# Six paired front pieces and a one-function 1/deviation tail in a one-layer decoder kernel

## The chip, the cores and the metric

The kernel runs on one core of a Trainium2 chip. The metric is the device time of one execution in microseconds (us); the figures here are the median of three runs. Engines are named as the profile names them: PE (TensorE matmuls; PEld its weight loads), DVE (VectorE), ACT (ScalarE), POOL (GpSimd) and SP (SyncE, which here only issues DMAs; ACT issues a few too).

## The reference

One layer of a decoder, for 256 prompt positions and 8 x 4 sample positions together (T = 288 columns), width D = 2048, in fp32:

```
z  = x @ w_in                       -> h, gate_b, gate_c, q, k, v, g_a, g_b
ya = gate_b * conv3(gate_c * h);  yb = merged dilated attention(q, k, v)
x1 = LN1(ALPHA*x  + (sigmoid(g_a)*(ya@w_a) + sigmoid(g_b)*(yb@w_b)) @ w_out)
y  = LN2(ALPHA*x1 + (silu(conv3(x1@w_up_a)) * (x1@w_up_b)) @ w_down)
LN(u) = (u - mean(u)) * rsqrt(var(u) + 1e-5) * g + b     over the 2048 features
```

The key and value caches and convolution states are outputs as well.

## The kernel before, in words

**Layout and products.** Activations lie feature-major: 128 partitions x 16 blocks of features (KD = 16) x 288 tokens. A weight block is 128 output features, 128x2048 fp32, 1 MiB in memory. Every fp32 product is made of three matmuls per 128x128 tile: operands are split into a rounded part (`hi`, a ScalarE cast) and the rest (`lo`, a VectorE subtraction), and `mms` (L188) adds hi·xh, hi·xl and lo·xh in PSUM. A block takes 48 matmuls of 288 columns.

**The stream of weights.** `prepare` (L161) issues a block's DMA on SP into `wst` (three buffers), and `half_block` (L134) casts (L137) and subtracts (L138) its two halves into `whi` and `wlo` (four buffers each). `product` (L174) takes a ready block, prepares the next and multiplies. The order on each engine is set by a scheduler that works from its own estimate of times; `tc.issue_after` and `behind` pin some instructions behind others.

**The front.** Twenty matmuls on zeros (L213) run while the first data come. x comes in four pieces (`FIRST`, L66: feature blocks 0-1, 2-7, 8-11, 12-15) by DMAs that ACT issues (L221); the first two weight blocks come in the same four pieces each, by DMAs that SP issues (L232), into two `wst` buffers. For every piece ACT casts and DVE subtracts the weights of each block (L234, L235) and x (L200, L201, in `split`). The product loop for q (L433) multiplies the first two blocks one after the other, interleaved by the scheduler. Behind the front's DMAs SP issues the third block, then constants (`cst`, `m_dist` into tile `yal`), the fourth block and parameters (`prm`), in the first three products (L436-438). A DMA carries one of eight completion semaphores in turn, so the ninth and later DMAs wait for the one eight places before.

**The tail.** The last products add into `dd`; `Norm.add` (L556) keeps sums of dd and of its square on POOL; two pairs of matmuls on a matrix of 1/D (L572, L573) spread mean and mean square over all partitions in PSUM (`p1`, `p2`). `finish_out` (L593) computes v = variance + eps (L600, DVE), then r = v^-1/2 as Ln (L608) and Exp (L609) on ACT, a Newton step (L614 ACT, L616 and L617 DVE, giving `dev` in PSUM) and a copy for POOL (L618). Over the 16 feature blocks it subtracts the mean (L604: blocks 0-8 on DVE in three passes, 9-15 on POOL), multiplies by dev (L604: 0-10 on DVE in four passes, 11-15 on POOL), and applies gain and bias (L630 on ACT for 0-8, 14, 15; L628 on DVE for 9-13). SP sends y in six pieces (L631). The first norm, `finish` (L578), uses the same Ln and Exp (L584, L585) and feeds the `w_up` products.

Of the kernel before, what the change touches and what calls it, by code (L numbers as in the profile page):

```python
# [11 lines left out]
F32R = mybir.dt.float32r  # L12
AF = mybir.ActivationFunctionType
ALU = mybir.AluOpType
# [3 lines left out]
P = 128  # L18
D = 2048
KD = D // P  # L20
# [6 lines left out]
H = T // 2  # L27
# [4 lines left out]
HK = KD // 2  # L32
# [18 lines left out]
C_M0 = C_TM + NT  # L51
# [11 lines left out]
N_CT = 18  # L63
N_REST = 48

FIRST = ((0, 2), (2, 6), (8, 4), (12, 4))  # L66

N_WARM = 20


N_STEP = N_CT + 2
N_STEP_BLOCKS = 2 * NG * NH + 5 * KD - 3

MEAN_DVE = ((0, 3), (3, 3), (6, 3))
MEAN_POOL = ((9, 1), (10, 2), (12, 2), (14, 2))
OUT_DVE = ((0, 1), (1, 3), (4, 3), (7, 4))
OUT_POOL = ((11, 1), (12, 2), (14, 2))
OUT_ORDER = ((0, 1), (1, 3), (4, 3), (7, 4), (11, 3), (14, 2))
OUT_LAST = (9, 10, 11, 12, 13)


@with_exitstack
def layer_kernel(ctx: ExitStack, tc: tile.TileContext, ins, outs):
    nc = tc.nc
    pe, dve, act, pool, sp = nc.tensor, nc.vector, nc.scalar, nc.gpsimd, nc.sync

    big = ctx.enter_context(tc.tile_pool(name="big", bufs=1))
    wp = ctx.enter_context(tc.tile_pool(name="wp", bufs=3))
    wk = ctx.enter_context(tc.tile_pool(name="wk", bufs=2))
# [8 lines left out]
    def sb(pl, shape, tag, dt=F32, bufs=None):  # L98
        return pl.tile(shape, dt, tag=tag, name=nm(tag), bufs=bufs)

    def acc(half=H):
        return sb(ps, [P, half, 2], "acc")

    def h2(ap):
        return ap.rearrange("p (h a) -> p h a", h=2)

    def h3(ap):
        return ap.rearrange("p k (h a) -> p k h a", h=2)
# [4 lines left out]
    def f32(ap):  # L113
        return ap.bitcast(F32)
# [3 lines left out]
    w_load = [None]  # L118
# [5 lines left out]
    def behind(i, after):  # L124

        tc.add_manual_dep(i.ins, after.ins.name, no_sync, reason="pace")
# [34 lines left out]
    def prepare():  # L161
        src, nk = next(w_left, (None, 0))
        if nk == 0:
            return
        st = sb(wp, [P, KD, P], "wst")
        d = sp.dma_start(st[:, :nk, :], src.rearrange("p (k c) -> p k c", c=P))
        loads[0] += 1
        n = loads[0]
        w_load[0] = d
        if n > NB_QKV + 5 * KD and n % 11 in (0, 4, 8):  # L170
            copy_rest(d)
        w_ready.append([half_block(st, k0, min(HK, nk - k0)) for k0 in range(0, nk, HK)])

    def product(x):  # L174

        w = w_ready.pop(0)
        if not w_ready:
            prepare()
        if steps_on[0]:
            spent[0] += N_STEP  # L180
            while spent[0] >= N_STEP_BLOCKS:
                spent[0] -= N_STEP_BLOCKS
                next(steps, None)
        o = acc(x[0].shape[-1])
        mms(o, w, x)
        return o.rearrange("p a h -> p h a")
# [12 lines left out]
    def split(hi, lo, src):  # L199
        act.copy(hi, src)  # L200
        dve.tensor_tensor(lo, src, f32(hi), ALU.subtract)  # L201
# [15 lines left out]
    xl = sb(big, [P, KD, 2, HX], "xl", F32R)  # L217
    x_in = ins["x"].rearrange("p (k t) -> p k t", t=T)
    xs = sb(big, [P, KD, T], "yah")
    for k0, n in FIRST:  # L220
        act.dma_start(xs[:, k0 : k0 + n, :], x_in[:, k0 : k0 + n, :])  # L221
    w_ready = []
    stage = []
    for b in range(2):
        stage.append((sb(wp, [P, KD, P], "wst"), ins["w_in"][b].rearrange("p (k c) -> p k c", c=P)))
        halves = [[sb(wp, [P, HK, P], n, F32R, bufs=4) for n in ("whi", "wlo")] + [HK] for _ in range(2)]
        w_ready.append(halves)
    for k0, n in FIRST:
        k = slice(k0, k0 + n)
        h = slice(k0 % HK, k0 % HK + n)  # L230
        for b, (st, src) in enumerate(stage):
            sp.dma_start(st[:, k, :], src[:, k, :])  # L232
            hi, lo, _ = w_ready[b][k0 // HK]
            act.copy(hi[:, h, :], st[:, k, :])  # L234
            dve.tensor_tensor(lo[:, h, :], st[:, k, :], f32(hi[:, h, :]), ALU.subtract)  # L235
            if b == 0:
                split(xh[:, k, :, :H], xl[:, k, :, :H], h3(xs[:, k]))
    x = (xh[:, :, :, :H], xl[:, :, :, :H])
    x_gb = (xh[:, :, :, :HG], xl[:, :, :, :HG])

    cst = sb(big, [P, C_M0], "cst")

# [187 lines left out]


    kv = sb(big, [P, 2, 2, NG, T], "dd")
    for j in range(NH):  # L433
        for g in range(NG):
            act.copy(h2(q_all[:, j, g]), product(x))
            if j == 0 and g > 0:  # L436
                for dst, src in ((cst, ins["cst"][:, :C_M0]), (m_dist, ins["cst"][:, C_M0:])) if g == 1 else ((prm, ins["prm"]),):
                    behind(sp.dma_start(dst, src), w_load[0])
        pool.tensor_copy(q_s[:, :, j, :], q_all[:, j, :, SEQ:])
    steps_on[0] = True  # L440
    for j in range(NH):
# [100 lines left out]
    class Norm:  # L542
# [13 lines left out]
        def add(self, i):  # L556
            d = dd[:, i]
            last = i == KD - 1
            q = self.s2 if i == 0 else sb(wk, [P, T], "cy", bufs=2)
            act.activation(q, d, AF.Square)  # L560
            if i == 0:
                pool.tensor_copy(self.s1, d)
            elif not last:
                pool.tensor_tensor(self.s1, self.s1, d, ALU.add)
                pool.tensor_tensor(self.s2, self.s2, q, ALU.add)
            if i == KD - 2:

                act.activation(lw[:, 3, 0:1], q[:, 0:1], AF.Ln)
            if last:
                self.p1, self.p2 = att(T), att(T)  # L570
                for p, s, e in ((self.p1, self.s1, d), (self.p2, self.s2, q)):
                    pe.matmul(p, ones_d, s, start=True, stop=False)  # L572
                    pe.matmul(p, ones_d, e, start=False, stop=True)  # L573
# [4 lines left out]
        def finish(self):  # L578

            mu, v, r, t = (lw[:, k] for k in range(3, 7))  # L580
            act.copy(mu, self.p1)
            act.activation(t, self.p1, AF.Square)
            dve.scalar_tensor_tensor(v, self.p2, EPS, t, ALU.add, ALU.subtract)
            act.activation(t, v, AF.Ln)  # L584
            act.activation(r, t, AF.Exp, scale=-0.5)  # L585

            dve.tensor_tensor(t, r, r, ALU.mult)
            dve.scalar_tensor_tensor(t, t, -0.5, v, ALU.mult, ALU.mult)
            dve.scalar_tensor_tensor(r, t, 1.5, r, ALU.add, ALU.mult)
            dve.scalar_tensor_tensor(mu, mu, -1.0, r, ALU.mult, ALU.mult)  # L590
            self.r, self.nmr = r, mu

        def finish_out(self, y, out):  # L593

            mu, r_pool, t = (lw[:, k] for k in range(3, 6))
            mean, v = self.p1, self.p2
            r, dev = (sb(ps, [P, T], tag, bufs=n) for tag, n in (("acc", None), ("long", 1)))
            act.activation(t, mean, AF.Square)
            act.copy(mu, mean)
            i_v = dve.scalar_tensor_tensor(v, v, EPS, t, ALU.add, ALU.subtract)  # L600

            def by_token(eng, k0, n, w, op):
                k = slice(k0, k0 + n)
                return eng.tensor_tensor(dd[:, k], dd[:, k], w.unsqueeze(1).broadcast_to([P, n, T]), op)  # L604

            for k0, n in MEAN_POOL:
                by_token(pool, k0, n, mu, ALU.subtract)
            act.activation(t, v, AF.Ln)  # L608
            act.activation(r, t, AF.Exp, scale=-0.5)  # L609
            with tc.issue_after(i_v.ins):  # L610
                for k0, n in MEAN_DVE:
                    i_m = by_token(dve, k0, n, mean, ALU.subtract)

            act.activation(t, r, AF.Square)  # L614
            with tc.issue_after(i_m.ins):
                dve.scalar_tensor_tensor(t, t, -0.5, v, ALU.mult, ALU.mult)  # L616
                i_r = dve.scalar_tensor_tensor(dev, t, 1.5, r, ALU.add, ALU.mult)  # L617
            act.copy(r_pool, dev)  # L618
            for k0, n in OUT_POOL:
                by_token(pool, k0, n, r_pool, ALU.mult)  # L620
            with tc.issue_after(i_r.ins):
                for k0, n in OUT_DVE:
                    i_m = by_token(dve, k0, n, dev, ALU.mult)
            for k0, n in OUT_ORDER:
                for i in range(k0, k0 + n):
                    if i in OUT_LAST:
                        with tc.issue_after(i_m.ins):
                            dve.tensor_scalar(y[:, i], dd[:, i], self.at(self.g, i), self.at(self.b, i), ALU.mult, ALU.add)  # L628
                    else:
                        act.activation(y[:, i], dd[:, i], AF.Identity, bias=self.at(self.b, i), scale=self.at(self.g, i))  # L630
                sp.dma_start(out[:, k0 : k0 + n, :], y[:, k0 : k0 + n, :])  # L631
# [267 lines left out]
```

## Time and profile before

| what | us |
|---|---|
| median of 3 runs (lowest to highest) | 1771.77 (1770.14 to 1772.48) |
| the profiled execution | 1772.71 |
| its span, first to last instruction | 1770.9 |
| PE busy in the span | 1749.3 (99%), 14277 matmul records |
| DVE, ACT, POOL busy | 1010.0, 800.8, 252.4 |
| mean granted TensorE clock | 0.995 of full speed |

The page gives busy time by engine, the chain of work that ended last, and the costliest groups by line. The trace behind it can be asked for the instructions of a stretch in order of time, for what an engine waited for, and for busy time, granted clock and DMA rate by stretch. Times within it count from the span's start. A busy PE is not a PE at its peak: a matmul's record is longer than the spacing of matmuls.

### The profile page before, as it was taken

Reading aid. Unit: us, or ns where it says so; the run is one execution under the profiler, and the core shown is the slowest. Engines: PE = TensorE matmul, PEld = TensorE weight load, DVE = VectorE, ACT = ScalarE, POOL = GpSimd, SP = SyncE. Lnnn points to the kernel's source line nnn. Section 1 sums busy time; section 2 is a strip of 40 time slices with the busy share of each in tenths; the row PEclk is TensorE's granted clock in tenths of the full one; section 3 lists DMA queues with packets and bytes.
Section 4 is the critical chain, followed back from the end, with each engine's and each line's share of the span. In section 5 each row is a group of like instructions: output and inputs, shape, how many; then the busy total and the mean of one; then the engine's idle time right before and its main releaser. Section 6 shows DMA issues by size and latency. Waiting matters only on the chain.

```text
span 1770.9 us, 33606 instructions
## 1 busy us (share of the span) xinstructions
PE 1749.3 (99%) x14277; PEld 1717.1 (97%) x14277; DVE 1010.0 (57%) x1321; ACT 800.8 (45%) x1178; POOL 252.4 (14%) x402
## 2 busy tenths in 40 slices
PE   8999999999999999999999999999999999999996
PEld 8999899999999999999999999999999999999996
DVE  4445446555645444455688787774555554555564
ACT  5444434333434333344455655553444443345444
POOL 0000000000000000001255233320011110011174
PEclk9999999999999999999999999999999999999998
DMA  8476677788787787467766566666666666666652
GB/s 305 172 301 258 258 292 272 288 304 316 260 322 301 296 322 264 151 247 270 283 218 235 214 226 226 226 226 223 229 227 226 230 222 233 219 236 219 242 191 104
DMA packets 59430, 436.25 MB, mean 246 GB/s; under 512 B 7184, under 2 KB 7696, under 8 KB 15248
## 3 DMA queue, kind: packets, MB, share of 16 engines
q1 hardware_dynamic: 57552, 428.22, 66.1%
q10 hardware_dynamic: 1728, 5.90, 0.9%
q8 instruction: 111, 1.82, 0.4%
q14 instruction: 39, 0.32, 0.0%
HBM read 389.89 MB, written 94.53 MB: 274 GB/s over the span
## 4 chain that ended last, share of the span: by engine, by line
PE 97%; ACT 1%; DVE 1%; DMA 0%; POOL 0%; issue 0%; ACTq 0%; DVEq 0%
PE acc L194 31%; PE acc L196 31%; PE acc L195 31%; PE long L356 1%; PE long L407 1%; DMA yah<-in_x 0%; PE att L283 0%; PE att L302 0%; ACT yah L630 0%; POOL qk_s L478 0%; DVE dd L604 0%; PE att L298 0%; ACT whi L137 0%; ACT xh L200 0%; PE att L276 0%
## 5 line engine op out<-in xcount | busy, mean ns | idle before, releaser
L138 DVE TENSOR_TENSOR wlo<-wst,whi 128x1024 fp32r<-128x1024 f32 (+1 forms) x580 | 710.5, 1225 | 608.0 <-ACT whi L137 602.1
L137 ACT CAST whi<-wst 128x1024 fp32r<-128x1024 f32 (+1 forms) x580 | 592.3, 1022 | 864.3 <-PE acc L195 763.6
L194 PE MATMUL acc<-xh,whi 128*128 128x288 f32 (+1 forms) x3264 | 940.1, 288 | 2.7 <-ACT whi L234 2.7
L196 PE MATMUL acc<-xh,wlo 128*128 128x288 f32 (+1 forms) x3264 | 937.3, 287 | 0.3 <-DVE wlo L235 0.3
L195 PE MATMUL acc<-xl,whi 128*128 128x288 f32 (+1 forms) x3264 | 936.3, 287 | 0.9 <-DVE xl L201 0.9
L194 PEld LDWEIGHTS acc<-xh,whi 128*128 128x128 f32 x3264 | 618.1, 189 | 14.0 <-issue 3.8
L196 PEld LDWEIGHTS acc<-xh,wlo 128*128 128x128 f32 x3264 | 618.1, 189 | 1.7 <-issue 0.8
L195 PEld LDWEIGHTS acc<-xl,whi 128*128 128x128 f32 x3264 | 618.3, 189 | 1.5 <-DVE xl L201 1.1
L194 PE MATMUL acc<-yah,whi 128*128 128x288 f32 x1216 | 348.2, 287 | 0.3 <-ACT yah L200 0.3
L196 PE MATMUL acc<-yah,wlo 128*128 128x288 f32 x1216 | 347.8, 286 | 0.0
L195 PE MATMUL acc<-yal,whi 128*128 128x288 f32 x1216 | 347.6, 286 | 0.0
L194 PEld LDWEIGHTS acc<-yah,whi 128*128 128x128 f32 x1216 | 229.7, 189 | 3.2 <-ACT h L519 2.5
L195 PEld LDWEIGHTS acc<-yal,whi 128*128 128x128 f32 x1216 | 229.8, 189 | 0.1
L196 PEld LDWEIGHTS acc<-yah,wlo 128*128 128x128 f32 x1216 | 229.8, 189 | 0.1
L478 POOL COPY qk_s<-u 128x2 f32<-128x2 f32 x44 | 41.7, 947 | 573.7 <-ACT u L680 441.5
L464 DVE SCALAR_TENSOR_TENSOR cy<-u,prm,cy 128x304 f32<-128x304 f32 x120 | 71.2, 594 | 3.3 <-ACT cy L462 0.6
L534 POOL TENSOR_TENSOR ya<-ya,dd 128x288 f32<-128x288 f32 x16 | 13.6, 849 | 306.0 <-DVE ya L533 306.0
L489 DVE TENSOR_TENSOR ya<-cy,acc 128x144 f32<-128x144 f32 x132 | 25.7, 249 | 33.0 <-PE acc L196 33.0
L478 POOL COPY cm<-u 128x2 f32<-128x2 f32 x16 | 3.0, 185 | 257.2 <-DVE u L505 257.2
L200 ACT CAST yah<-ya 128x288 fp32r<-128x288 f32 x76 | 32.7, 431 | 15.1 <-POOL ya L534 8.4
L201 DVE TENSOR_TENSOR yal<-ya,yah 128x288 fp32r<-128x288 f32 x76 | 34.9, 460 | 1.1 <-ACT yah L200 1.1
L462 ACT ACTIVATE cy<-u,prm 128x304 f32<-128x304 f32 x60 | 32.9, 549 | 3.1
(158 smaller groups left out, 791.8 us busy)
## 6 DMA issues: line engine op xcount, KB each, us to landing
wst<-in_w_in SPq DMA_DIRECT2D x114, 1024.0 KB, 6.1
wst<-in_w_up SPq DMA_DIRECT2D x88, 1024.0 KB, 4.8
wst<-in_w_down SPq DMA_DIRECT2D x32, 1024.0 KB, 4.9
cache<-in_ck SPq DMA_DIRECT2D x18, 1024.0 KB, 6.4
out_o_ck<-cache SPq DMA_DIRECT2D x18, 1024.0 KB, 9.2
cache<-in_cv SPq DMA_DIRECT2D x18, 1024.0 KB, 6.3
out_o_cv<-cache SPq DMA_DIRECT2D x18, 1024.0 KB, 9.9
wst<-in_w_a SPq DMA_DIRECT2D x16, 1024.0 KB, 4.9
```

The costliest lines, as they stand in the source:

```text
L137: act.copy(hi[:, :n, :], st[:, k0 : k0 + n, :])
L138: dve.tensor_tensor(lo[:, :n, :], st[:, k0 : k0 + n, :], f32(hi[:, :n, :]), ALU.subtract)
L194: pe.matmul(out, hi[:, c, :], xh_k, start=k == 0, stop=False)
L195: pe.matmul(out, hi[:, c, :], xl_k, start=False, stop=False)
L196: pe.matmul(out, lo[:, c, :], xh_k, start=False, stop=k == nk - 1)
L200: act.copy(hi, src)
L201: dve.tensor_tensor(lo, src, f32(hi), ALU.subtract)
L356: pe.matmul(p[j * NS : (j + 1) * NS], qm[:, j, b, :], c[:, o + j * cols : o + (j + 1) * cols], start=b == 0, stop=b == NB - 1,)
L462: act.activation(y, u[:, :YW], AF.Copy, scale=prm[:, w0 : w0 + 1])
L464: dve.scalar_tensor_tensor(y, u[:, i : i + YW], prm[:, w0 + i : w0 + i + 1], y, ALU.mult, ALU.add)
L478: pool.tensor_copy(dst[:, 0:2], u[:, SEQ : SEQ + 2])
L489: dve.tensor_tensor(a, b, c, ALU.mult)
```

## The change

In the front, x comes in six pieces (four of two feature blocks by ACT's DMAs, two of four by SP's), and both first weight blocks come together, one DMA for a piece of both, into one tile that borrows `dd`; hi goes into the tile `yal`, lo into two `cache` buffers. The casts and subtractions take both blocks at once. `first_two` multiplies piece by piece, term by term, alternating the two blocks, in an order that is pinned. The third block's load comes right behind the front's DMAs, and `cst`, `m_dist` and `prm` are issued three products later. There are 18 matmuls on zeros.

In the tail, r is one ACT function, `Abs_reciprocal_sqrt`, of v (in `finish` too), with the Newton step kept; its table is asked for where Ln's was. DVE's mean and dev passes take turns over the same blocks, and shares move: mean 0-7 on DVE and 8-15 on POOL; dev 0-11 on DVE and 12-15 on POOL; gain and bias 8-11 on DVE, the rest on ACT. The output pieces are 3, 3, 2, 4, 2 and 2 blocks.

In the compiled program the rest of the order on every engine is the same. On ACT the front's casts come in the order x0, w0, w1, x1, w2, x2, w3, x3, x4, w4, x5, w5 (w: both blocks of a piece), on DVE the subtractions likewise; on SP `cst` comes behind the fifth block, `m_dist` behind the sixth and waits for PE, `prm` behind the seventh. On ACT the tail's blocks come in the order 0-5, 12, 13, 6, 7, 14, 15.

```diff
-FIRST = ((0, 2), (2, 6), (8, 4), (12, 4))
-N_WARM = 20
+FIRST = ((0, 2, "act"), (2, 2, "act"), (4, 2, "act"), (6, 2, "act"), (8, 4, "sp"), (12, 4, "sp"))
+N_WARM = 18
-MEAN_DVE = ((0, 3), (3, 3), (6, 3))
-MEAN_POOL = ((9, 1), (10, 2), (12, 2), (14, 2))
-OUT_DVE = ((0, 1), (1, 3), (4, 3), (7, 4))
-OUT_POOL = ((11, 1), (12, 2), (14, 2))
-OUT_ORDER = ((0, 1), (1, 3), (4, 3), (7, 4), (11, 3), (14, 2))
-OUT_LAST = (9, 10, 11, 12, 13)
+NORM_DVE = ("m", 0, 3), ("r", 0, 3), ("m", 3, 3), ("r", 3, 3), ("m", 6, 2), ("r", 6, 2), ("r", 8, 2), ("r", 10, 2)
+MEAN_POOL = (8, 2), (10, 2), (12, 2), (14, 2)
+OUT_POOL = (12, 2), (14, 2)
+GB_DVE = (8, 9, 10, 11)
+OUT_ORDER = (0, 3), (3, 3), (6, 2), (8, 4), (12, 2), (14, 2)
...
-    for k0, n in FIRST:
-        act.dma_start(xs[:, k0 : k0 + n, :], x_in[:, k0 : k0 + n, :])
...
-            sp.dma_start(st[:, k, :], src[:, k, :])
-            hi, lo, _ = w_ready[b][k0 // HK]
-            act.copy(hi[:, h, :], st[:, k, :])
-            dve.tensor_tensor(lo[:, h, :], st[:, k, :], f32(hi[:, h, :]), ALU.subtract)
-            if b == 0:
-                split(xh[:, k, :, :H], xl[:, k, :, :H], h3(xs[:, k]))
+    w_two = sb(big, [P, 2, KD, P], "dd")
+    w_two_hi = sb(big, [P, 2, KD, P], "yal", F32R)
+    w_two_lo = [sb(wk, [P, 2, HK, P], "cache", F32R, bufs=2) for _ in range(2)]
+    w_in_two = ins["w_in"][0:2].rearrange("b p (k c) -> p b k c", c=P)
+    for k0, n, queue in FIRST:
+        k = slice(k0, k0 + n)
+        (act if queue == "act" else sp).dma_start(xs[:, k], x_in[:, k])
+        sp.dma_start(w_two[:, :, k], w_in_two[:, :, k])
+    for k0, n, _ in FIRST:
+        k = slice(k0, k0 + n)
+        split(xh[:, k, :, :H], xl[:, k, :, :H], h3(xs[:, k]))
+        split(w_two_hi[:, :, k], w_two_lo[k0 // HK][:, :, k0 % HK : k0 % HK + n], w_two[:, :, k])
+    def first_two():
+        prepare()
+        o = [acc() for _ in range(2)]
+        before = None
+        for k0, n, _ in FIRST:
+            for term in range(3):
+                for k in range(k0, k0 + n):
+                    xk = x[term == 1][:, k].rearrange("p h a -> p a h")
+                    for b in range(2):
+                        w = w_two_lo[k // HK][:, b, k % HK] if term == 2 else w_two_hi[:, b, k]
+                        i = pe.matmul(
+                            o[b], w, xk, start=k == 0 and term == 0, stop=k == KD - 1 and term == 2
+                        )
+                        if before is not None:
+                            behind(i, before)
+                        before = i
+        return [t.rearrange("p a h -> p h a") for t in o]
...
+    q_first = first_two()
-            act.copy(h2(q_all[:, j, g]), product(x))
-            if j == 0 and g > 0:
-                for dst, src in ((cst, ins["cst"][:, :C_M0]), (m_dist, ins["cst"][:, C_M0:])) if g == 1 else ((prm, ins["prm"]),):
-                    behind(sp.dma_start(dst, src), w_load[0])
+            act.copy(h2(q_all[:, j, g]), q_first.pop(0) if q_first else product(x))
+            if j == 1:
+                dst, src = ((cst, ins["cst"][:, :C_M0]), (m_dist, ins["cst"][:, C_M0:]), (prm, ins["prm"]))[g]
+                behind(sp.dma_start(dst, src), w_load[0])
...
-                act.activation(lw[:, 3, 0:1], q[:, 0:1], AF.Ln)
+                act.activation(lw[:, 3, 0:1], q[:, 0:1], AF.Abs_reciprocal_sqrt)
...
-            act.activation(t, v, AF.Ln)
-            act.activation(r, t, AF.Exp, scale=-0.5)
+            act.activation(r, v, AF.Abs_reciprocal_sqrt)
...
+            before = i_v
+            for n_op, (what, k0, n) in enumerate(NORM_DVE):
+                with tc.issue_after(before.ins):
+                    before = by_token(dve, k0, n, *((mean, ALU.subtract) if what == "m" else (dev, ALU.mult)))
+                if n_op == 0:
+                    with tc.issue_after(before.ins):
+                        dve.scalar_tensor_tensor(t, t, -0.5, v, ALU.mult, ALU.mult)
+                        before = dve.scalar_tensor_tensor(dev, t, 1.5, r, ALU.add, ALU.mult)
+                    act.copy(r_pool, dev)
```

## The prediction

> **What bounds the kernel now.** I read the page first, then PE's waits, then the first 30 us and the last 20 us in order of time. On the page:
>
> ```profile
> PE 1749.3 (99%) x14277; PEld 1717.1 (97%) x14277; DVE 1010.0 (57%) x1321; ACT 800.8 (45%) x1178; POOL 252.4 (14%) x402
> ...
> PE 97%; ACT 1%; DVE 1%; DMA 0%; POOL 0%; issue 0%; ACTq 0%; DVEq 0%
> ```
>
> PE is the bound, and between 30 and 1740 us its waits come to 0.3 us. So only the two ends can be shortened. ACT's casts that wait for PE's buffers start at 31.12 and 37.01, one block of 48 matmuls apart: 5.89 us, or 0.1226 us a matmul at full clock. PE's busy time and clock in the front, by the view of stretches (length, busy, count, clock, DMA share, GB/s):
>
> ```profile
> 4.60:8.00 3.40, 2.38 (x19) 1.00 1.02 417
> 8.00:11.40 3.40, 0.88 (x5) 0.98 1.02 409
> 11.40:14.75 3.35, 3.09 (x12) 0.50 1.05 387
> 14.75:18.10 3.35, 3.35 (x16) 0.50 1.01 413
> ```
>
> PE starves from 8 to 11.4, then works until 18.1 at half clock, 0.24 us a matmul, before it is back at full. The ACT and DVE rows beside it:
>
> ```profile
> 18.06 1.05 ACT L137 CAST whi<-wst 128x1024 fp32r<-128x1024 f32 x1 [1.96 <-DMA wst<-in_w_in]
> ...
> 25.37 0.40 ACT L435 COPY yah<-acc 128x288 f32<-128x288 f32 x1 [2.30 <-PE acc L196]
> ...
> 19.14 1.23 DVE L138 TENSOR_TENSOR wlo<-wst,whi 128x1024 fp32r<-128x1024 f32 x1 [1.27 <-ACT whi L137]
> ```
>
> L435 at 25.37 copies the second product. Its last matmul, the 96th, started about 0.3 us earlier (a matmul's record is 0.29 long), at 25.05. Had PE run at full clock without a gap, it would have begun at 25.05 - 95 x 0.1226 = **13.4**. I call this the equivalent start: what moves it moves the end. L137 and L138 show the other limit: the third block is in memory at 18.03, its first `lo` half ready at 20.37, when PE has not yet come to it.
>
> In the tail:
>
> ```profile
> 1755.74 1.28 ACT L609 ACT_TABLE_LOAD   x1
> ...
> 1757.11 1.04 DVE L604 TENSOR_TENSOR dd<-dd,att 128x864 f32<-128x864 f32 x1
> 1758.08 0.45 DVE L616 SCALAR_TENSOR_TENSOR cache<-cache,att 128x288 f32<-128x288 f32 x1
> 1758.56 0.46 DVE L617 SCALAR_TENSOR_TENSOR long<-cache,acc 128x288 f32<-128x288 f32 x1
> ...
> 1764.26 0.33 SPq L631 DMA_DIRECT2D out_o_y<-yah  x1
> ...
> 1765.00:1769.40 4.40, 0.00 (x0) 0.00 (x0) 0.00 (x0) 1.23 (x3) 0.00 (x0) 0.50 1.00 401
> ```
>
> Newton's step waits for DVE's third mean pass, not for the table: Exp and Square are done at 1757.89. At the end ACT's last block is done at 1766.23, but the queue writes without a gap from 1765.0 to 1769.4, and the span ends 1.5 later: the last four pieces, issued from 1764.26 on, are 12 blocks of 147 KB, 1.77 MB, 4.4 us at 401 GB/s. DMA ends the kernel, fed by the passes.
>
> **Front, step by step.** Bytes first. Third block and everything ahead of it are 2.36 (x) + 2.10 + 1.05 = 5.5 MB before and after; `cst` and `m_dist` were issued behind it and move further back. So it lands at 18.0 again, if short rows cost nothing. The first four paired pieces (1.05 MB) have 1 KB rows; the nearest row is the first output piece (1152-byte rows), 357 GB/s in its best 0.3 us against about 410: 0.0 to 0.4 us more. I take 18.2. Then ACT 1.05, DVE 1.23, handovers: first `lo` half at 20.55. PE can have done 98 matmuls by then; equivalent start 20.55 - 98 x 0.1226 = **8.5**.
>
> Is the rest ready? I share the measured rate between the queues by row length (2304 bytes of x to 1024 of w) and take 0.9 of it for the slowest part of a transfer; done for the kernel before, this gives 12.2 for the last x piece and 18.0 for the third block (ACT took them at 12.30 and 18.06). Estimated landings after: x0 4.1, w0 5.4, w1 7.7, w2 8.4, w3 9.2, x4 10.8, w4 12.3, x5 13.9, w5 15.3. ACT takes 0.67 (x) and 0.62 (w) for small pieces, 1.15 and 1.05 for large; DVE 0.76, 0.69, 1.35, 1.23 (rows of these sizes in L200, L201, L235, L137 and L138; 512 elements for w0-w3). ACT's order puts x1 behind w1, so x1, there at 5.3, is cast at 8.9. PE ends the six pieces at 7.6, 10.7, 12.2, 13.7, 16.6 and 19.5. That is 1.0 before block three's `lo`, so block three decides. Gain **13.4 - 8.5 = 4.9**. With the measured rate whole and no loss on short rows the same sum gives 7.2; with 0.87 and 15% loss, 9.3: gain 4.1 to 6.2.
>
> Two fewer matmuls on zeros: nothing, as PE then waits for w0 until 6.1 (about 0.25 us if it didn't). Matmuls, bytes and later weight loads are the same in number. `m_dist` now waits on SP until PE ends the pair (19.5), ahead of the seventh block and `prm`. The seventh block is due at 8.5 + 6 x 5.89 = 43.8 and takes about 8 us from issue: hidden, with some 15 us of cover; beyond that each us costs one. `prm` heads ACT's cast for that same block: same cover. The first norm loses a load and a pass (1.28 + 0.45 at 978 us); only DVE waited (1.1 us), PE didn't: 0.
>
> **Tail, step by step.** v is ready at 1755.28. Abs_reciprocal_sqrt has no row; ACT's passes over 288 elements take 0.39 to 0.44 without pointers and 0.63 with: I take 0.41. Square follows 0.45 later and ends at 1756.17, when DVE ends its first mean pass. Newton 0.94, copy 0.4: first dev pass at 1757.60 instead of 1759.48, **1.9 earlier**, with the mean passes of five blocks still to come. DVE in turn (3 blocks 0.96, 2 blocks 0.67 apart, 1.05 and 0.75 where the next waits for its result): blocks 0-2 done 1758.65, 3-5 1760.69, 6-7 1762.14, then 8-11 1763.48, gain and bias (0.34 apart, first 0.43) until 1764.95. Before: 1764.92. POOL has twelve blocks either way, 1.36 a pair: 12-13 at 1761.9, 14-15 at 1763.25. ACT at 0.52 a block: 0-2 until 1760.35, 3-5 1762.4, 12-13 1763.4, 6-7 1764.45, 14-15 1765.5: 0.75 earlier than before. The last three pieces are issued at 1764.5, 1764.95 and 1765.5; first bytes 0.8 after issue (as 1764.26 to 1765.07 before), 1.18 MB at 401 GB/s: 1768.2 against 1769.4. Gain **1.2**; 0.5 if each hand-over on DVE costs 0.2 more, 1.7 if the last piece finds the queue empty.
>
> On the table the row and a page differ. The trace has a load for Ln (L568) and one for Exp (L609), 1.28 us, and Exp starts 0.01 after the latter. The Trainium skill, page "ScalarE: Activation LUTs", section "What ACT_TABLE_LOAD costs", gives about 2.66 us with a drain, and its section "Table sets: the hidden batching unit" has Ln and Exp share one set. By 2.66 a removed load would be worth 1.4 us more than the row; the trace shows neither drain nor sharing.
>
> **The sum** is 4.9 + 1.2 = 6.1 against the profiled execution: 1772.71 - 6.1 = 1766.6. That execution lay 0.94 over the median; if all of this is profiling, 1765.7. Part of it may be the front's own stall, so I give **1766.0**.
>
> **Rivals.**
> - *The clock falls all the same.* In the four stretches above PE kept full clock after 70% busy, lost it after 26%, and didn't regain it after 92%. Afterwards PE is busy 43 to 63% in any 3.4 us between 5.2 and 11.4, in between, and full after. Half clock from 11.4 to 14.8 gives an equivalent start of 9.4, from 8 to 14.8 10.4, from 8 to 18.1 12.0: 1767 to 1769.5, middle 1768.3. The Trainium skill, page "TensorE: Matmul & The Clock Gate", section "Part 1: The HAM clock gate", has a free-running window of about 3.4 us, an idle one of which halves the clock. By it the phase differs from run to run, and no window here is idle. The trace agrees on the length (changes at 4.6, 11.4, 18.1).
> - *Slower: half clock through the whole front.* If the thin first pieces drop the clock at 5 us and gaps hold it down, 96 matmuls at 0.24 from 6.1 end at 29.1: equivalent start 17.8, and 13.4 - 17.8 + 1.2 = -3.2: 1775.0 with the 0.94 taken off, 1775.9 without. It decides if half clock lasts past about 23 us. Against it: from 10.6 on the casts feed PE faster than half clock eats.
> - *The tail gives nothing* (ACT's in-order 12-13 or DVE's turns late): 1767.2.
> - *The front doesn't get faster*, the paired loads with 1 KB rows running far under 350 GB/s: only the tail, 1770.6. For it: 103 to 210 GB/s between 2.4 and 3.6 us; against: over 340 from 4 us on with the same rows among them.
>
> **How the numbers follow.** Forecast 0.68, fallen clock 0.17, tail nothing 0.07, front nothing 0.04, slower 0.04. The measurement can tell about 0.2% (3.5 us) from no change: below 1768.2 is faster. The forecast, the tail rival and half of the fallen clock lie there: 0.80; slower by over 0.2% (1775.3) half of the slower rival, 0.02; same 0.18. The range, 1763.2 to 1769.2, takes 7.9 us (6.2 + 1.7) at the low end and the fallen clock's three-quarter point at the high.
>
> **What would show it.** Right: clock 1.00 throughout the front; first copy of q near 19.7 instead of 22.67; third block's first subtraction ending near 20.5 with PE waiting for it about 1 us; no table load between v and r; first dev pass 2.3 us after v; last block on ACT about 10.2 after v. Wrong: PEclk 0.5 anywhere before 20 us; weight pieces landing 1 us late or more; a PE wait on `whi` after 25 us; output pieces written with gaps at the end.

## The result and the profile after

The changed kernel takes **1766.56 us** (median of 8 runs, 1766.45 to 1766.66); the kernel before, measured beside it, 1771.49 (8 runs, 1769.95 to 1772.48). The ratio is 0.9973, 95% interval 0.9962 to 0.9984: 4.9 us less. The profiled execution after took 1766.61, with a span of 1764.8 and a clock of 0.997. Against the profiled execution before, 1772.71, that is 6.1, the sum of the prediction; against the medians it is 4.9. The difference comes from before: its runs lie 2.5 us apart, those after 0.2.

The page of the changed kernel, PE's busy time and the chain that ended last by engine:

```profile
PE 1747.1 (99%) x14275; PEld 1714.4 (97%) x14275; DVE 1009.9 (57%) x1321; ACT 797.5 (45%) x1175; POOL 253.8 (14%) x401
...
PE 97%; DMA 1%; ACT 1%; DVE 1%; POOL 0%; issue 0%; SPq 0%; ACTq 0%; DVEq 0%
```

PE is still the bound. The same four stretches of the front (length, PE busy, count, clock, DMA share, GB/s):

```profile
4.60:8.00 3.40, 3.12 (x19) 1.00 1.04 367
8.00:11.40 3.40, 2.73 (x16) 1.00 1.04 398
11.40:14.75 3.35, 3.29 (x27) 1.00 1.07 416
14.75:18.10 3.35, 3.35 (x30) 1.00 1.02 424
```

The hole from 8 to 11.4, 0.88 us busy before, is 2.73 busy now, and the two rows with 0.50 are gone. PE's rows in order of time (start, length from first to last, instruction, count, idle time before and who ended it):

```profile
5.92 0.80 PE L249 MATMUL acc<-xh,yal 128*128 128x288 f32 x4
...
7.97 0.76 PE L249 MATMUL acc<-xh,yal 128*128 128x288 f32 x4 [0.27 <-ACT xh L201]
...
10.64 0.76 PE L249 MATMUL acc<-xh,yal 128*128 128x288 f32 x4 [0.60 <-ACT xh L201]
...
18.91 1.14 PE L249 MATMUL acc<-xh,cache 128*128 128x288 f32 x8
19.89 0.29 PE L195 MATMUL acc<-xh,whi 128*128 128x288 f32 x1
20.01 0.29 PE L196 MATMUL acc<-xl,whi 128*128 128x288 f32 x1
20.35 0.39 PE L197 MATMUL acc<-xh,wlo 128*128 128x288 f32 x1
```

L249 is the pair, L195 to L197 the third block. The pair's 96 matmuls would take 11.8 us at 0.1226; they take 13.97, from 5.92 to 19.89. The 2.2 us more lie nearly all ahead of 11.5, in waits for ACT's casts of pieces 1 and 2 and the DVE subtractions behind them. At the third block's first `lo` PE loses 0.2 us. ACT and DVE beside it:

```profile
6.72 0.62 ACT L201 CAST yal<-dd 128x512 fp32r<-128x512 f32 x1 [0.86 <-DMA dd<-in_w_in]
7.25 0.67 ACT L201 CAST xh<-yah 128x576 fp32r<-128x576 f32 x1
9.39 0.62 ACT L201 CAST yal<-dd 128x512 fp32r<-128x512 f32 x1 [1.48 <-DMA dd<-in_w_in]
...
17.99 1.99 ACT L138 CAST whi<-wst 128x1024 fp32r<-128x1024 f32 x2 [1.45 <-DMA wst<-in_w_in]
19.97 0.70 ACT L452 COPY yah<-acc 128x288 f32<-128x288 f32 x2
...
19.07 2.36 DVE L139 TENSOR_TENSOR wlo<-wst,whi 128x1024 fp32r<-128x1024 f32 x2 [1.23 <-ACT whi L138]
```

Pieces are counted from 0. ACT can start on the weights of piece 1 (`yal<-dd`) at 6.72 and on those of piece 2 at 9.39; it stands idle before both, with x1 queued behind w1. It starts on the third block at 17.99; that block's first subtraction is the first half of the last row, done at 20.30. L452 copies the first product at 19.97 (22.67 before).

The tail, ACT and DVE from v on (L616 starts at 1749.85, takes 0.47 us and gives v at 1750.32):

```profile
1750.35 0.40 ACT L622 ACTIVATE acc<-att 128x288 f32<-128x288 f32 x1 [0.36 <-DVE att L616]
1750.77 0.41 ACT L623 ACTIVATE cache<-acc 128x288 f32<-128x288 f32 x1
...
1750.22 1.04 DVE L620 TENSOR_TENSOR dd<-dd,att 128x864 f32<-128x864 f32 x1
1751.22 0.46 DVE L633 SCALAR_TENSOR_TENSOR cache<-cache,att 128x288 f32<-128x288 f32 x1
1751.71 0.46 DVE L634 SCALAR_TENSOR_TENSOR long<-cache,acc 128x288 f32<-128x288 f32 x1
1752.63 1.05 DVE L620 TENSOR_TENSOR dd<-dd,long 128x864 f32<-128x864 f32 x1 [0.47 <-ACT cache L635]
```

And the stretch in which the last outputs are written (busy of PE, PEld, DVE, ACT, POOL, then clock, DMA share, GB/s):

```profile
1760.40:1763.40 3.00, 0.00 (x0) 0.00 (x0) 0.00 (x0) 0.15 (x1) 0.00 (x0) 0.50 0.99 388
```

No table load stands between v and r (L622), Newton's step (L633, L634) starts behind one mean pass instead of three, the first dev pass comes 2.3 us after v (4.2 before), and from 1760.4 on the queue writes without a gap, as before.

### The profile page after: what moved, and what is told of

Read it like the earlier page. It is cut to its first block, busy times and chain, and to the rows that moved or that the text cites. A ratio compares the mean times of both kernels' runs of the same rounds, so it can differ in the third digit from the quotient of the medians.

```text
span 1764.8 us, 33592 instructions
## 1 busy us (share of the span) xinstructions
PE 1747.1 (99%) x14275; PEld 1714.4 (97%) x14275; DVE 1009.9 (57%) x1321; ACT 797.5 (45%) x1175; POOL 253.8 (14%) x401
## 4 chain that ended last, share of the span: by engine, by line
PE 97%; DMA 1%; ACT 1%; DVE 1%; POOL 0%; issue 0%; SPq 0%; ACTq 0%; DVEq 0%
PE acc L195 31%; PE acc L197 31%; PE acc L196 31%; PE long L372 1%; PE long L423 1%; DMA wst<-in_w_in 0%; PE att L299 0%; PE att L318 0%; DMA dd<-in_w_in 0%; ACT whi L138 0%; POOL qk_s L495 0%; ACT yah L644 0%; DVE dd L620 0%; PE att L314 0%; ACT xh L201 0%; PE att L292 0%
## 5 line engine op out<-in xcount | busy, mean ns | idle before, releaser
L195 PE MATMUL acc<-xh,whi 128*128 128x288 f32 (+1 forms) x3232 | 929.5, 288 | 0.0
L197 PE MATMUL acc<-xh,wlo 128*128 128x288 f32 (+1 forms) x3232 | 927.0, 287 | 0.0
L196 PE MATMUL acc<-xl,whi 128*128 128x288 f32 (+1 forms) x3232 | 925.7, 286 | 0.0
L195 PEld LDWEIGHTS acc<-xh,whi 128*128 128x128 f32 x3232 | 610.9, 189 | 10.9 <-issue 3.8
L197 PEld LDWEIGHTS acc<-xh,wlo 128*128 128x128 f32 x3232 | 610.9, 189 | 1.3 <-issue 0.8
L196 PEld LDWEIGHTS acc<-xl,whi 128*128 128x128 f32 x3232 | 610.9, 189 | 0.4 <-issue 0.2
L195 PE MATMUL acc<-yah,whi 128*128 128x288 f32 x1216 | 348.2, 287 | 0.3 <-ACT yah L201 0.3
L197 PE MATMUL acc<-yah,wlo 128*128 128x288 f32 x1216 | 347.8, 286 | 0.0
L195 PEld LDWEIGHTS acc<-yah,whi 128*128 128x128 f32 x1216 | 229.7, 189 | 3.2 <-ACT h L536 2.5
L197 PEld LDWEIGHTS acc<-yah,wlo 128*128 128x128 f32 x1216 | 229.8, 189 | 0.1
L581 POOL TENSOR_TENSOR cache<-cache,dd 128x288 f32<-128x288 f32 x28 | 27.7, 990 | 46.5 <-DVE dd L660 31.5
```

The lines of the kernel that those rows point to most:

```text
L195: pe.matmul(out, hi[:, c, :], xh_k, start=k == 0, stop=False)
L196: pe.matmul(out, hi[:, c, :], xl_k, start=False, stop=False)
L197: pe.matmul(out, lo[:, c, :], xh_k, start=False, stop=k == nk - 1)
```

## The experiments

A measure that the clock of the front doesn't touch helps with the tail: from ACT's Square of the mean (the first instruction that reads PE's last statistics) to the end of the span. Its start is also the marker of how early PE finished.

| kernel | start of the Square | span | tail |
|---|---|---|---|
| before | 1754.25 | 1770.9 | 16.65 |
| tail_only | 1754.20 | 1769.8 | 15.6 |
| front_only | 1749.00 | 1765.7 | 16.7 |
| rsqrt_old_order | 1749.05 | 1765.7 | 16.65 |
| turns_ln_exp | 1749.17 | 1766.5 | 17.3 |
| after | 1749.28 | 1764.8 | 15.5 |

### The front alone

The changed front with both norms of before:

```diff
-            act.activation(r, v, AF.Abs_reciprocal_sqrt)
+            act.activation(t, v, AF.Ln)
+            act.activation(r, t, AF.Exp, scale=-0.5)
...
-NORM_DVE = ("m", 0, 3), ("r", 0, 3), ("m", 3, 3), ("r", 3, 3), ("m", 6, 2), ("r", 6, 2), ("r", 8, 2), ("r", 10, 2)
+MEAN_DVE = ((0, 3), (3, 3), (6, 3))
+OUT_DVE = ((0, 1), (1, 3), (4, 3), (7, 4))
```

> The changed front with the tail and both norms of before. If the two ends add up: equivalent start of PE 8.4 as in the changed kernel, tail as before (16.2 us from the last matmul of the norm to the end of the span against 15.1), so a span of 1765.9 and about 1767.7 us, with the narrow spread of the changed kernel (0.2 us) if the spread of before comes from its front. Rival, that the tail's changes did part of the work ahead of the last product too: a span of 1766.5 or more.

Measured: 1767.49 (1767.39 to 1767.79) beside 1771.79 for before, ratio 0.9975 [0.9965, 0.9985]. The front gives 4.3 of the 4.9 us between the medians, 5.2 between the two profiled spans, and the narrow spread.

### The tail alone

The front of before with the changed tail:

```diff
-FIRST = ((0, 2, "act"), (2, 2, "act"), (4, 2, "act"), (6, 2, "act"), (8, 4, "sp"), (12, 4, "sp"))
-N_WARM = 18
+FIRST = ((0, 2), (2, 6), (8, 4), (12, 4))
+N_WARM = 20
...
-    q_first = first_two()
```

> The front of before with the changed tail. If the ends add up: 1.1 us less than the kernel before in the profile's tail (15.1 us from the last matmul of the norm), 1770.4 in the median, with the wide spread of before (2.5 us), since the front's clock still falls. Rival, that the spread belongs to the tail: a spread under 0.5 us.

Measured: 1770.40 (1768.63 to 1771.75), ratio 0.9992 [0.9982, 1.0001]; the interval includes no change, since the spread of before stays with its front. In the trace the tail is 15.6 against 16.65, 1.05 less. Its front has the same fall of the clock as before, a little earlier.

### One function for 1/deviation, the passes in the old order

```diff
-            before = i_v
-            for n_op, (what, k0, n) in enumerate(NORM_DVE):
...
+            with tc.issue_after(i_v.ins):
+                for k0, n in MEAN_DVE:
+                    i_m = by_token(dve, k0, n, mean, ALU.subtract)
```

> Changed front, 1/deviation in one function, but the passes of the tail in the order and shares of before. My theory, that Newton's step waited for DVE's third mean pass and not for the table: first dev pass 4.2 us after v as before, and the tail within 0.1 us of the front-only kernel: 1767.7. Rival, that the table load was on the path: 1.3 to 1.7 us earlier in the tail, 1766.0 to 1766.4.

Measured: 1767.65 (1767.34 to 1767.86), 0.9977 [0.9968, 0.9986], within the ranges of front_only (1767.49). ACT and DVE of this run:

```profile
1750.54 0.41 ACT L630 ACTIVATE cache<-acc 128x288 f32<-128x288 f32 x1
...
1749.99 2.97 DVE L621 TENSOR_TENSOR dd<-dd,att 128x864 f32<-128x864 f32 x3
1752.88 0.45 DVE L632 SCALAR_TENSOR_TENSOR cache<-cache,att 128x288 f32<-128x288 f32 x1
```

ACT is done with r and its square at 1750.95, and Newton's step starts at 1752.88, when DVE has ended its third mean pass. The table load that went was hidden behind that pass: alone, its removal is worth nothing.

### The passes in turn, with Ln and Exp

```diff
-            act.activation(r, v, AF.Abs_reciprocal_sqrt)
+            act.activation(t, v, AF.Ln)
+            act.activation(r, t, AF.Exp, scale=-0.5)
```

> The changed kernel with Ln and Exp, and their table load, in place of the one function; passes in turn. My theory: with only one mean pass ahead of Newton's step DVE now waits for the table, 1.7 us; dev comes 1.7 later than in the changed kernel, and the end with it by 1.0 to 1.7 us, 1767.6 to 1768.3, no better than the old order or worse. Rival, that turns alone bring the gain: 1766.6 to 1766.9.

Measured: 1768.34 (1768.1 to 1768.68), 0.9981 [0.9971, 0.999]: 0.85 slower than front_only. ACT and DVE:

```profile
1750.66 1.28 ACT L624 ACT_TABLE_LOAD   x1
...
1752.84 0.45 DVE L635 SCALAR_TENSOR_TENSOR cache<-cache,att 128x288 f32<-128x288 f32 x1 [1.69 <-ACT cache L625]
```

Now DVE waits 1.69 us for Exp and the square (L625), with its other passes pinned behind. So the two halves of the tail gain only together: alone one gives 0 and the other costs 0.85, both give 0.9. This run also prices the load, which is now on the path: 1768.34 - 1766.56 = 1.8, and the load with the second function makes 1.28 + 0.43 = 1.7. By the 2.66 with a drain that the Trainium skill states (page "ScalarE: Activation LUTs", section "What ACT_TABLE_LOAD costs") it would, as an estimate, have been 3.1; the measurement decides for the row.

### The gap filled: what the clock is worth

The kernel before, with 27 matmuls on zeros pinned into PE's gaps (16, 7 and 4 ahead of the three matmuls of the third feature block); nobody reads their product:

```diff
+FILL = (16, 7, 4)
...
+                    if first and k == 2:
+                        for _ in range(FILL[term]):
+                            fill = pe.matmul(o_fill, zero[:, :P], zero, start=True, stop=True)
+                            behind(fill, last)
+                            last = fill
```

> The kernel before with 27 more matmuls on zeros (16, 7 and 4) pinned into the three gaps of PE between the first and the second piece; they add work that nothing reads. Theory that the fallen clock is the larger part of the front's loss: full clock throughout, equivalent start near 10.4 instead of 13.4, about 3 us off the profiled span (1767.9), the rest up to 8.4 left to the paired, finer pieces. The time would also lose its spread. Rival, that PE was starved by arrival and its clock didn't matter: no change, 1771.5, or slower by the added matmuls.

Measured: 1769.90 (1769.79 to 1770.06) beside 1771.65, 0.9989 [0.998, 0.9999]; span 1768.1 against 1770.9. The two stretches that decided:

```profile
8.00:11.40 3.40, 3.40 (x28) 1.00 1.02 413
11.40:14.75 3.35, 3.35 (x26) 1.00 1.05 394
```

With PE busy on zeros the clock stays full and the spread falls from 2.5 us and more to 0.3. The shortest of before's times beside it (1769.85) lies within the range of fill_gap. So of the 5.0 us by which the changed front is earlier in the trace (Square 1754.25 to 1749.28), at least 2.8 are the fallen clock, and with it goes the spread of before. Between the medians it is 1.75 of the 4.3 that the front gives, since the profiled execution of before lay 0.94 over its median.

Up to 2.2 us are left, and the trace shows where they lie. In fill_gap the last wait of PE is for the second piece, of six feature blocks:

```profile
9.33 1.96 DVE L213 TENSOR_TENSOR xl<-yah,xh 128x1728 fp32r<-128x1728 f32 x1 [2.25 <-ACT xh L212]
...
12.43 0.29 PE L205 MATMUL acc<-xh,whi 128*128 128x288 f32 x1
```

That piece of x is subtracted only at 11.29, the weights beside it at 12.15, and the matmul at 12.43 is PE's 16th on the two blocks; from there on it has no gap. In the changed kernel, with pieces of two feature blocks, 36 are done by 12.54. The 16th at 12.43 is an equivalent start of 12.43 - 15 x 0.1226 = 10.6, 2.2 us behind the 8.4 of the changed kernel.

### One matmul on zeros instead of 18

```diff
-N_WARM = 18
+N_WARM = 1
```

> The changed kernel with 1 matmul on zeros instead of 18. Theory of the clock: PE meets the pieces at half clock, regains full clock only after a window filled with work, between 14.8 and 21.5 us; equivalent start 10.4 to 13.7 instead of 8.4, so 1768.6 to 1771.9, with a wider spread. Rival, that arrival alone decides: 1766.6.

Measured: 1766.61 (1766.46 to 1767.16), 0.9971 [0.9959, 0.9982]: no change, against the theory and for its rival. PE:

```profile
6.01 1.32 PE L249 MATMUL acc<-xh,yal 128*128 128x288 f32 x4 [4.18 <-ACT yal L201]
...
9.05 1.16 PE L249 MATMUL acc<-xh,yal 128*128 128x288 f32 x4
10.01 0.74 PE L249 MATMUL acc<-xl,yal 128*128 128x288 f32 x4
...
19.89 0.29 PE L195 MATMUL acc<-xh,whi 128*128 128x288 f32 x1
```

Until 10.1 four matmuls take about 0.96 us from start to start, 0.24 each, half the pace; from there 0.1226. Yet PE reaches the third block at 19.89, the same as with the warm-up. Slow matmuls filled the time in which the changed kernel waits: here PE works without a gap from 6.01, and 13.88 - 11.77 = 2.1 us of slowness stand for the 2.2 us of waits. Ahead of 11.5 the pair would wait about 2 us at full clock, so a full clock there gains nothing.

### The third block in two halves

```diff
-        d = sp.dma_start(st[:, :nk, :], src.rearrange("p (k c) -> p k c", c=P))
+        src3 = src.rearrange("p (k c) -> p k c", c=P)
+        for k0, n in ((0, HK), (HK, HK)) if loads[0] == 0 else ((0, nk),):
+            d = sp.dma_start(st[:, k0 : k0 + n, :], src3[:, k0 : k0 + n, :])
```

> The changed kernel with the third block loaded by two DMAs of half a block. My theory, that the pair's end on PE (19.8) and the third block's first subtraction (20.3, for the third matmul after the pair) lie 0.2 us apart: 0.2 us gained, no more, 1766.3. Rival, that the third block's landing is the bound by a whole microsecond as the prediction had it: 1.0 to 1.3 gained, 1765.3 to 1765.6.

Measured: 1766.26 (1766.18 to 1766.65), 0.997 [0.9958, 0.9982]. ACT casts the first half 1.2 us earlier, and PE walks into the third block without the 0.2 us gap:

```profile
16.82 1.05 ACT L138 CAST whi<-wst 128x1024 fp32r<-128x1024 f32 x1 [0.23 <-DMA wst<-in_w_in]
...
19.84 0.29 PE L197 MATMUL acc<-xh,whi 128*128 128x288 f32 x1
19.96 0.29 PE L198 MATMUL acc<-xl,whi 128*128 128x288 f32 x1
20.08 0.29 PE L199 MATMUL acc<-xh,wlo 128*128 128x288 f32 x1
```

The median is 0.3 lower; the ranges overlap, so the size is not sure, but the gap is seen to go. The pair itself ends at 19.84, not earlier.

### A finer last piece

```diff
-FIRST = (... (8, 4, "sp"), (12, 4, "sp"))
+FIRST = (... (8, 4, "sp"), (12, 2, "sp"), (14, 2, "sp"))
```

> The changed kernel with the last piece of four feature blocks cut into two of two. The pair should end on PE 1.2 to 1.5 us earlier, and the third block still lands at 17.9: if that is the other bound, 0.0 gained or up to 0.3 lost to smaller rows, 1766.5 to 1766.9. Rival, that the pair's end is the bound: 1.2 gained, 1765.4.

Measured: 1766.99 (1766.84 to 1767.38), 0.9974 [0.9963, 0.9984]: 0.4 slower. The pair's end did not move (19.97): PE has work in store from 11.5 on, so when the last piece comes doesn't matter. But the third block came later (ACT's cast at 18.32 instead of 17.99), and PE took its first `lo` at 20.68 instead of 20.35. The DMA engines were busy throughout (share 1.06 from 10.4 to 14.0), but moved 388 GB/s there against 409 in the changed kernel, and the third block's load was issued at 10.33 instead of 9.39. Which of the two, the shorter rows or the later issue, delayed the block is not shown.

### The casts with x ahead of the weights

ACT's and DVE's work on every piece pinned behind the one before, x first (`seen` holds the last cast and subtraction):

```diff
+            two = act.copy(hi, src), dve.tensor_tensor(lo, src, f32(hi), ALU.subtract)
+            if seen:
+                for i, j in zip(two, seen[-1]):
+                    behind(i, j)
+            seen.append(two)
```

> The changed kernel with one thing different: in every piece ScalarE casts x before the weights (and VectorE subtracts in that order), where the scheduler put w1 before x1 and w2 before x2. Theory: in the changed kernel ScalarE waits for w1 until 6.72 and for w2 until 9.39 and casts x1 and x2 only behind them, so PE gets pieces 1 and 2 about 0.6 us later than the weights allow; from 11.46 us on PE has a backlog, so the pair's end moves by the same 0.6, from 19.89 to about 19.3. But the third block's first remainder comes at 20.30 us whatever PE does, so PE waits there and the time stays at 1766.5 to 1766.7. Rival: the pair's end decides, the wait for the remainder is covered, and the time falls by 0.6 to 1766.0.

Measured: 1766.56 (1766.29 to 1766.72), 0.997 [0.9959, 0.9982], as the theory had it, but only half for its reason. ACT and PE:

```profile
12.62 1.05 ACT L238 CAST yal<-dd 128x1024 fp32r<-128x1024 f32 x1 [0.19 <-DMA dd<-in_w_in]
...
13.72 1.25 PE L257 MATMUL acc<-xh,yal 128*128 128x288 f32 x8 [0.56 <-ACT yal L238]
...
19.71 0.29 PE L195 MATMUL acc<-xh,whi 128*128 128x288 f32 x1
...
20.26 0.39 PE L197 MATMUL acc<-xh,wlo 128*128 128x288 f32 x1
```

PE starts piece 1 at 7.57 instead of 7.97 and piece 2 at 9.96 instead of 10.64, and then runs out of work before piece 4: its weights land at 12.6, and PE waits 0.56 us for their cast. Of the 0.6 us that were to come at the pair's end 0.2 are left, and the wait for `lo` takes those.

### The order and the halves

> The same order of casts, and the third block's load in two halves as well (which alone gave 1766.26, with the first remainder at 17.89 us). Theory: with both waits gone the pair's end at about 19.3 us goes through to the third block without a gap, and the time is 0.6 less than with the halves alone: 1765.6 to 1765.8. Rival: the early gaps on PE are set by the landing of w1 and w2 and not by the order of the casts; then it is 1766.2 to 1766.3 as with the halves alone.

Both edits above together. Measured: 1766.08 (1765.91 to 1766.36), 0.9968 [0.9956, 0.998]. This is the fastest kernel of the study, its slowest run below the fastest of the changed kernel, but the gain over the halves alone is 0.2, not 0.6, and the ranges of these two overlap. PE again waits for piece 4 (0.51 us before 13.66) and enters the third block at 19.64 without a gap. The landing of that piece's weights is what is left.

### Block by block

All loads, casts and pieces as changed; PE takes the six pieces of block 0 and then those of block 1:

```diff
-        for k0, n, _ in FIRST:
-            for term in range(3):
-                for k in range(k0, k0 + n):
...
-                    for b in range(2):
+        for b in range(2):
+            for k0, n, _ in FIRST:
+                for term in range(3):
+                    for k in range(k0, k0 + n):
```

> The changed kernel with the same loads, casts and pieces, but PE takes all six pieces of block 0 and then all six of block 1. Theory: the pieces alone are worth little, and it is the second block that gives PE work to do while data arrive; block 0 alone has 48 matmuls of 0.143 us, 6.9 us of work for the time until the last piece is cast at 16.5 us, so PE ends block 0 at about 18.3 and block 1 6.9 later, at 25.1, 5.2 behind the changed kernel: 1771.8, and up to 1773.9 and spread if the clock falls in the gaps as well. Rival: the small first pieces bring the gain by an earlier start, and the order of the matmuls behind them is worth under 1 us: 1766.6 to 1767.6.

Measured: 1770.68 (1770.58 to 1771.11), 0.9994 [0.9985, 1.0003]. PE by stretch, then in order of time:

```profile
6.60:10.00 3.40, 2.05 (x12) 1.00 1.07 392
10.10:10.40 0.30, 0.00 (x1) 0.50 1.10 440
13.40:16.80 3.40, 3.40 (x16) 0.50 1.05 419
```

```profile
16.67 0.77 PE L249 MATMUL acc<-xh,yal 128*128 128x288 f32 x4
...
18.29 0.41 PE L249 MATMUL acc<-xh,yal 128*128 128x288 f32 x2
...
24.17 0.29 PE L195 MATMUL acc<-xh,whi 128*128 128x288 f32 x1
```

Block 0 ends at 18.29 and block 1 takes 5.88 more: PE comes to the third block 4.3 us later than in the changed kernel, which then loses 0.2 there, and the time is 4.1 more. So the six pieces are worth nothing that these runs can tell when the second block's matmuls do not stand between (tail_only, with the old front, 1770.40). The theory's size was too large because it took 0.143 us a matmul and not 0.1226; with that it gives 24.2. The clock fell here too, and that cost little: block 0's last piece is cast only at 16.36 and subtracted at 17.64, and PE takes it at 16.67 and 17.77. Nor did this fall spread the times, which lie 0.5 us apart in ten runs.

This does not make the second block's matmuls the thing that the change added. The kernel before multiplies both blocks while data arrive, too:

```profile
22.67 0.40 ACT L435 COPY yah<-acc 128x288 f32<-128x288 f32 x1 [2.02 <-PE acc L196]
```

It copies the first product at 22.67 and the second at 25.37, 2.7 us or 22 matmuls apart, so 26 of the second block's 48 matmuls came before the first block's last. Both blocks in large pieces (tail_only) and small pieces one block after the other (this run) thus take nearly the same time, and only small pieces with both blocks gain. No run changes the size of the pieces alone, the paired loads alone or the pinned order alone, so their shares stay open; the rows of fill_gap speak for the size of the pieces.

## Why the prediction came out right, and where it did not

**The sum** is confirmed as it was made, against the profiled execution: 4.9 + 1.2 = 6.1 forecast, 4.97 + 1.15 measured (Square 1754.25 to 1749.28; tail 16.65 to 15.5), 1766.6 against 1766.61.

**The step from 1766.6 to 1766.0 failed.** The 0.94 us by which the profiled execution lay over the median was put down in part to profiling. Profiling costs nothing that can be seen: after, the profiled execution is 1766.61 and the median 1766.56. The 0.94 was the front's own spread. The runs with the old front lie 2.5 to 3.2 us apart (before, tail_only), all those with the changed front 0.2 to 0.7, and fill_gap narrows the old front itself to 0.3. The gain to be had on the median was therefore smaller than on that execution, while the time after was the plain sum.

**The front.** "Block three decides" holds by a hair only. Its `lo` was ready at 20.30 for the 20.55 of the estimate, and PE was to have waited 1 us for it; it waited 0.2. The term that was mis-sized is the pair's own end, 19.5 forecast and 19.89 measured: w2 was estimated to land at 8.4 and ACT could start on it only at 9.39, with x2's cast behind it. As the pair's end did not decide, this error cost the forecast nothing: the equivalent start was 8.5 forecast and 13.4 - 5.0 = 8.4 measured. Had the pair ended 0.2 us later still, it would have decided. Three limits lie within 0.4 us: the landing of piece 4 (19.64 to 19.71 at the pair's end), the order of the casts (19.89), and the third block's `lo` (20.30 for the third matmul behind the pair, so 20.05 at the pair's end). This is why the halves give 0.3, the order 0.0, and both 0.5.

**The clock** stayed full, as the forecast had it, and fill_gap shows what that is worth: some 2.8 us in the trace. But two things said of it were too simple. The rival of a fallen clock gave every half-clock stretch a price; no_warm had 4.1 us of half pace, from 6.0 to 10.1, and lost nothing, since PE would have waited for as long. What a fall behind 11.5 costs the changed kernel, where PE has work in store, no run shows. And the fall doesn't need idleness: in block_by_block it came after a stretch with 2.05 of 3.40 us busy (60%), with no gap over 0.6 us in it, whereas in the changed kernel it held through 2.73 of 3.40 (80%). The limit can't be named from these runs: in tail_only the clock held through another stretch 60% busy (2.06 us from 4.18 to 7.59). The prediction's 43 to 63% for the changed front count 0.1226 us a matmul, while the 70, 26 and 92% that it sets them against are shares of records, each 0.29 us long; by records the front was 80 to 92% busy (2.73 and 3.12 of 3.40). The Trainium skill, page "TensorE: Matmul & The Clock Gate", section "Part 1: The HAM clock gate", has an idle window of about 3.4 us halve it. The lengths agree with such a window (half clock from 10.1 to 16.9 in block_by_block, from 11.3 to 18.1 before, twice 3.4); the idleness doesn't. That two fewer matmuls on zeros cost nothing held; 17 fewer cost nothing either.

**What was costed at nothing.** Between 25 and 1700 us PE's waits come to 0.3 us, as before: the later `cst`, `m_dist` and `prm` stayed hidden, and the first norm's load was worth nothing to PE.

**The tail** went by its steps: Abs_reciprocal_sqrt 0.40 us (0.41 taken), first dev pass 2.3 us after v (2.3), ACT's last block done 10.2 after v (10.2), the writes without a gap from 1760.4 to the end, 1.15 us in all for 1.2. That Newton's step waited for the third mean pass and not for the table is shown by rsqrt_old_order, and that the turns need the shorter function by turns_ln_exp.

**The rivals.** The front that doesn't get faster and the slower one are excluded by front_only, the tail that gives nothing by the 0.9 us between front_only and the changed kernel; the fallen clock did not occur. Three side sums of the prediction do not come out as written, and nothing hangs on them: the slower rival's end at 29.1 is an equivalent start of 17.4, not 17.8; the shares below 1768.2 add to 0.835, not 0.80; and 7.9 us off the median are 1763.9, not 1763.2.

## What to carry to other kernels

At a start where data trickle in, give PE independent work for every byte that has arrived (here a second block on the same x), and bring it in pieces small enough that the first of them can be worked on early: here large pieces with two blocks and small pieces one block after the other were equally slow, and only both together gained. Before you pay for a limit, write down when the next two would bind: here three lay within 0.4 us, and removing one alone gave 0.3 at most. And where a chain on one engine hides behind passes on another, shorten the chain and reorder the passes together: either alone gave nothing or a loss.

## What the runs showed that was not expected

- The clock fell after a stretch that was 60% busy, and came back only after 6.8 us, with PE working without a gap for all but the first 0.3 of them (block_by_block, 10.1 to 16.9).
- In no_warm the clock column shows 1.00 before 10.1, while matmuls stand 0.24 us apart: there the spacing tells the pace, and the column doesn't. The pace rose after 4.1 us of gapless work.
- The spread between runs came from the front: 2.5 to 3.2 us with the old one, 0.2 to 0.7 with the changed one, and 0.3 with the old one whose gaps were filled with work on zeros. A fallen clock alone does not make it: block_by_block had one, and 0.5.
